# x loaded in place with its gain applied in the splits, a priority on cross output's last tile, and the first retention output weight loaded ahead of its operands

## The chip, the core and the metric

The kernel runs on one core of a Trainium2 chip. The metric is the device time of one execution, in microseconds (us). The kernel before took 2256.48, 2258.14 and 2258.49 us in three runs; the median is 2258.14. The profile is of one more execution.

## What is computed

One inference step of a one-layer encoder, for a prompt of 1024 tokens and a sample of 64, D_MODEL = 1024, in float32:

```
xn = rms_norm(x, g);  xn @ w_in -> retention q|k|v|gate, SWA q|k|v, branch gates A|B
A  = retention(4 heads of 256), per-head norm, swish gate, @ w_ret_out
B  = sliding-window attention (16 heads of 64 on 2 KV heads, window 128), @ w_swa_out
x += (sigmoid(gate_a) * A + sigmoid(gate_b) * B) @ w_mix_out
x += cross_attention(rms_norm(x), memory of 256 tokens, 4 heads)
x += swiglu(rms_norm(x));   y = rms_norm(x)
```

Outputs are y, the retention states, the window's keys and values, and the memory's keys and values, for prompt and sample.

## The kernel before

**Numbers.** Every fp32 matmul operand is split into a hi and a lo part of type fp32r: `split` (L122) casts hi on ACT (L123) and subtracts on DVE for lo (L124). A product is three matmuls: hi x hi, hi x lo, lo x hi. A gain of a norm is one number per row of a transposed activation, that is, one per SBUF partition; `gained` (L269) applies it within a split: ACT multiplies and writes hi, DVE makes x*g - hi with one scalar_tensor_tensor.

**Layout.** Tokens stand in the free dimension: 8 tiles of 128 rows x 1088 tokens. For the projections and the feed-forward network the 1088 tokens are halved (HALF = 544, of 2 x HC = 272), and the products are Strassen's: 7 products (L205, L206, L208 are the matmuls of one) of weight operands P1 to P7 (built on POOL, L183 to L189) and activation operands B11, B12, B21, B22, T1 to T4. `put_op` splits one quarter of x into such an operand, and `put_sum` (L1280) first makes the difference of two quarters on DVE: T1 = B12 - B11, T2 = B22 - T1, T3 = T2 - B11, T4 = B21 - T2. The operands lie in two rings of eight slots. DVE adds the products from PSUM (u, L252).

**Stages.** Start and projections (0 to about 817 us): w_v by plain products, then w_k, w_q and the others by Strassen, with the retention heads (L691 to L815) between them. Mix (817 to 1240): sliding-window attention, and between its steps a filler that first does the last memory values (w_mv), then the retention output, w_ret_out. Cross attention (1240 to 1400), cross output (1400 to 1510), feed-forward (1510 to the end).

**The start** (`start_phase`). The 16 pieces of x (128 x 544) are loaded into four buffers `xr`; ACT multiplies each by its gain g into xg (L428), and with that frees the buffer for the next load. The first two w_v weights are loaded between the pieces. The operands are then split from xg: B11 and B12 after the second group of pieces, B21, B22, T1 (`first_sums`), T2, T3, T4 after the first weight's split. `token_squares` loads x once more for the norm's sums, which DVE adds (L452).

**Cross output** (`cross_out_phase`). For each of 8 rows of tiles and each of 3 chunks of tokens (384, 384, 320): load the residual, 24 matmuls, add the residual on DVE (L1241), store, apply the norm's gain (L1244), square and add the square into the norm's sum (L278). After the last row the norm's roots follow (`some_rstd`, L306).

**The filler** (`filler`). `operands` loads the gated retention outputs (d_gate, eight tiles per chunk) and splits them into `rets`. Each of these loads is pinned with issue_after behind the last weight load at that time (`self.loaded`, set in `unit_raw`). Then come the last memory values with weights that were loaded earlier (`first_units`), then for m = 0 to 7 `unit(w_ret_out[m])`, that is the load into a buffer `raw` (a pool of 2, 128 x 1024 each, shared by all weights), its split, and the products over the three chunks. The window attention's vT is loaded behind `operand_loaded`, the last d_gate load of the first chunk.

**Order.** All loads and stores go through SP's queue (L117), which issues in order. A scheduler at build time chooses each engine's order from the program's dependences and its own estimates; `tc.high_priority()` moves instructions forward in it, `tc.issue_after(i)` holds them behind i. The kernel waits for semaphores where tiles are reused.

Of the kernel before, what the change touches and what calls it, by code (L numbers as in the profile page):

```python
# [2 lines left out]

# [1 line left out]

# [6 lines left out]
F32 = mybir.dt.float32  # L12
F32R = mybir.dt.float32r
AF = mybir.ActivationFunctionType
ALU = mybir.AluOpType
# [4 lines left out]
P = 128  # L20
D = 1024
KT = D // P
# [18 lines left out]
HALF = T // 2  # L41
# [68 lines left out]
class Kernel:  # L110
# [295 lines left out]
    def start_phase(self, ctx):  # L406

        nc, tc, io = self.nc, self.tc, self.io
        g = self.gains[:, 0, :]
        xg = self.ring_tiles(0, KT // 2, "xg", F32)  # L410
        self.xg = [xg[k // 2][:, k % 2, :] for k in range(KT)]
        self.ops, self.slots = {}, {}
        self.new_b12(ctx)
        sp = ctx.enter_context(tc.tile_pool(name="sp", bufs=1, reuse_waits="tile"))
        self.early = [sp.tile([P, 2, HC], F32, name=f"early{i}") for i in range(4)]
        xr = lambda: sp.tile([P, HALF], F32, tag="xr", bufs=4, name="xr")
        raws = [self.wp.tile([P, 1024], F32, tag="raw", bufs=2, name="raw") for i in range(2)]

        def columns(j):
            for i in range(2):  # L420
                self.load(raws[i][:, j * 512:(j + 1) * 512].rearrange("p (k m) -> p k m", m=P), io["w_v"][i][:, 4 * j:4 * j + 4])

        def pieces(k0, t):
            hs = slice(t * HALF, (t + 1) * HALF)
            for k in range(k0, k0 + 4):
                x = xr()
                self.load(x, io["xT"][k, :, hs])
                nc.scalar.mul(self.xg[k][:, hs], x, g[:, k:k + 1])  # L428

        for n, (k0, t) in enumerate(((0, 0), (0, 1), (4, 0), (4, 1))):  # L430
            pieces(k0, t)
            if n < 2:
                columns(n)
            if n == 1:
                self.operands_early()
        self.load(self.ident, io["c_ident"])
        w = self.plain_weights(raws)
        self.operands_late(self.first_sums)
        return w

    def token_squares(self):

# [602 lines left out]
    def filler(self):  # L1045

        nc, tc, io = self.nc, self.tc, self.io
        if True:
            def ld():
                self.lds.append(self.lds.pop(0))  # L1050
                return self.lds[-1]

            rets = self.ring_tiles(1, KT, "ret")

            def operands(c0, n):
                after = self.loaded
                for k in range(KT):
                    a = ld()
                    with tc.issue_after(after):
                        ins = self.load(a[:, :n], self.d_gate[0][k, :, c0:c0 + n])  # L1060
                    if c0 == 0:
                        self.operand_loaded = ins
                    self.split(a[:, :n], rets[k][:, 0, c0:c0 + n], rets[k][:, 1, c0:c0 + n])

            for c0, n in CH:
                operands(c0, n)
            us, h = self.first_units, H - 1
            for t in range(2):
                ps = self.dense_psum()
                for k in range(KT):  # L1070
                    x = self.ms[k][:, :, t * P:(t + 1) * P]
                    self.mm3(ps[:, :256], x[:, 0], x[:, 1], *us[k // 4][k % 4], k == 0, k == KT - 1)
                    if k == 3:
                        yield
                o = ld()[:, :256]
                with tc.high_priority():
                    nc.scalar.mul(o, ps[:, :256], self.mtok[:, t:t + 1])
                self.store(self.d_mv[h, :, t, :], o)
                self.store(io["o_mv"][t * P:(t + 1) * P, h * 256:(h + 1) * 256], o)
                yield  # L1080
            for m in range(KT):
                u = self.unit(io["w_ret_out"][m], KT)
                for c0, n in CH:
                    g = ld()
                    self.load(g[:, :n], self.d_gate[1][m, :, c0:c0 + n])
                    for ps in self.pieces(u, rets, c0, n):
                        if ps is None:
                            yield
                    nc.vector.tensor_tensor(out=g[:, :n], in0=ps, in1=g[:, :n], op=ALU.mult)
                    self.store(self.d_mix[m, :, c0:c0 + n], g[:, :n])  # L1090
                    yield
# [130 lines left out]
    def cross_out_phase(self):  # L1222
        nc, tc, io = self.nc, self.tc, self.io
        with ExitStack() as ctx:
            cq = ctx.enter_context(tc.tile_pool(name="cq", bufs=1, reuse_waits="tile"))
            ctx.enter_context(self.plain_psum(side="right"))
            pn = ctx.enter_context(tc.tile_pool(name="pnc", bufs=1, reuse_waits="tile", space=PSUM, side="right"))
            self.norm_psum = lambda name: pn.tile([P, 512], F32, tag="n", name=name)
            xg = self.ring_tiles(0, KT // 2, "xg", F32)
            self.xg = [xg[k // 2][:, k % 2, :] for k in range(KT)]  # L1230
            self.ops, self.slots = {}, {}
            units = [lambda m=m: self.unit(io["w_co"][m], KT) for m in range(KT)]
            norms, rs = [], []
            for m, u, (c0, n) in self.m_major(units, CH, tail=2):
                if m == 4 and not self.ops:
                    self.operands_early()
                    self.first_sums()
                x = cq.tile([P, 384], F32, tag="hx", bufs=4, name="hx")[:, :n]
                self.load(x, self.d_h[0][m, :, c0:c0 + n])
                ps = self.dense(u, self.couts, c0, n)  # L1240
                nc.vector.tensor_tensor(out=x, in0=ps, in1=x, op=ALU.add)  # L1241
                self.store(self.d_h[1][m, :, c0:c0 + n], x)
                acc = self.rstd_f[:, c0:c0 + n]
                nc.vector.scalar_tensor_tensor(self.xg[m][:, c0:c0 + n], x, self.gains[:, 2, m:m + 1],  # L1244
                                               self.rstd[:, c0:c0 + n], ALU.mult, ALU.mult)
                self.add_square(acc, x, m == 0, cq, n)
                if m == KT - 1:
                    root = self.root[:, c0 // 384, :]
                    def first(acc=acc, root=root):
                        rs.append(self.some_rstd(acc, times=root))  # L1250

                    norms.append((first, lambda acc=acc, i=len(norms): self.spread(acc, rs[i])))
                    if len(norms) < 3:
                        self.later += norms[-1][:3 - len(norms)]
            self.later, self.last_roots = [norms[1][1], norms[2][1]], norms[2][0]
# [39 lines left out]
            b11, b12, _, _ = self.quarters(k)  # L1295
            self.put_sum("T1", k, b12, b12, b11)

    def operands_late(self, sums=None):
        self.op_tiles(1, ("B21", "B22", "T2", "T3"))
        qs = [self.quarters(k) for k in range(4)]  # L1300
        for k, (b11, b12, b21, b22) in enumerate(qs):
            self.put_op("B21", k, b21)
        for k, (b11, b12, b21, b22) in enumerate(qs):
            self.put_op("B22", k, b22)
        if sums is not None:
            sums()
        for k, (b11, b12, b21, b22) in enumerate(qs):
            self.put_sum("T2", k, b12, b22, b12)
        for k, (b11, b12, b21, b22) in enumerate(qs):
            self.put_sum("T3", k, b11, b12, b11)  # L1310
        self.op_tiles(0, ("T4",))
        for k, (b11, b12, b21, b22) in enumerate(qs):
            self.put_sum("T4", k, b21, b21, b12)
# [290 lines left out]
```

## Time and profile before

| | us |
|---|---|
| median of 3 runs | 2258.14 |
| profiled execution, its time | 2251.97 |
| profiled execution, its span | 2250.1 |
| PE busy | 2172.4 |
| DVE busy | 1594.2 |
| ACT busy | 896.2 |
| POOL busy | 689.0 |

The mean granted TensorE clock is 0.988 of full speed. PE is TensorE, DVE is VectorE, ACT is ScalarE, POOL is GpSimd, and SP issues the DMAs; PEq or SPq is an engine's sequencer. A row of a timeline gives start, duration, engine, line, operation, tiles (out<-in), shapes, and in brackets the idle time ahead of it and what ended that. A row of waits gives engine, tile, line, what it waited for, then the sum, the number and the longest. A row of a group by shape gives the sum, the mean in ns, and the idle time ahead. A row of windows gives the busy time and number of instructions of PE, PE's weight loads, DVE, ACT and POOL, the granted clock, the busy share of the DMA engines, and GB/s.

### The profile page before, as it was taken

The page shows a single profiled execution, that of the slowest core. Times are in us where ns is not written, and L with a number is a line of the kernel's source. Part 1 is how long each engine was busy: PE and PEld are TensorE (multiplying, and loading weights), DVE is VectorE, ACT ScalarE, POOL GpSimd, SP SyncE. Part 2 cuts the span into 40 slices and gives each one's busy share as a digit, 9 for nine tenths or more (in the row PEclk, how much of TensorE's full clock was granted, in tenths as well). Part 3 has the DMA queues.
Part 4 walks back from the last instruction along what each step waited for, and adds up shares of the span by engine and source line. Part 5 has one row for each costly group of instructions (what it writes and reads, how often), then busy time and mean ns, then how long its engine had stood idle before and what let it go on. Part 6 is the DMA issues. An engine that isn't in the chain of part 4 may idle for free.

```text
span 2250.1 us, 41674 instructions
## 1 busy us (share of the span) xinstructions
PE 2172.4 (97%) x16382; PEld 2108.2 (94%) x16382; DVE 1594.2 (71%) x2656; ACT 896.2 (40%) x1921; POOL 689.0 (31%) x466
## 2 busy tenths in 40 slices
PE   7899999999999989999999999999999999999996
PEld 6899999999999977779999998999999999999996
DVE  8985878677687568875455565776777767777596
ACT  7333333435444355553233343333222223344344
POOL 1441534342253112220000000014555556434471
PEclk9999999999999989999999999999999999999997
DMA  5433344443445475326343111412342332475223
GB/s 199 159 120 109 111 129 130 132 130 113 169 139 187 143 242 164 111 67 222 121 153 113 39 66 59 143 62 91 122 148 79 101 131 85 152 258 192 86 84 108
DMA packets 182598, 290.84 MB, mean 129 GB/s; under 512 B 40290, under 2 KB 110850, under 8 KB 182402
## 3 DMA queue, kind: packets, MB, share of 16 engines
q1 hardware_dynamic: 177794, 279.26, 38.2%
q10 hardware_dynamic: 4608, 8.91, 1.1%
q8 instruction: 129, 2.11, 0.4%
q14 instruction: 67, 0.55, 0.1%
HBM read 196.95 MB, written 91.16 MB: 128 GB/s over the span
## 4 chain that ended last, share of the span: by engine, by line
PE 80%; DVE 10%; DMA 4%; issue 3%; ACT 2%; POOL 1%; SPq 0%; DVEq 0%; ACTq 0%; POOLq 0%
PE pq L205 15%; PE pq L208 15%; PE pq L206 15%; PE pd L149 8%; PE pd L150 8%; PE pd L151 8%; DVE wq L124 2%; PE pout L992 1%; PE pp L976 1%; DMA hl<-d_op 1%; PE pss L934 1%; DVE T L124 1%; DVE B L124 1%; PE pk L691 1%; DVE xg L1280 1%
## 5 line engine op out<-in xcount | busy, mean ns | idle before, releaser
L123 ACT CAST wq<-raw 128x512 fp32r<-128x512 f32 (+1 forms) x505 | 307.9, 614 | 572.1 <-PE pq L208 308.2
L124 DVE TENSOR_TENSOR wq<-raw,wq 128x512 fp32r<-128x512 f32 (+1 forms) x505 | 447.6, 890 | 107.7 <-ACT wq L123 105.7
L205 PE MATMUL pq<-T,wq 128*128 128x272 f32 x1832 | 501.3, 291 | 6.4 <-DVE u L252 3.1
L206 PE MATMUL pq<-T,wq 128*128 128x272 f32 x1832 | 497.7, 288 | 0.0
L205 PE MATMUL pq<-B,wq 128*128 128x272 f32 x1592 | 436.7, 292 | 11.7 <-ACT wq L123 10.5
L206 PE MATMUL pq<-B,wq 128*128 128x272 f32 x1592 | 435.1, 290 | 9.1 <-DVE B L124 8.9
L208 PE MATMUL pq<-T,wq 128*128 128x272 f32 x1832 | 382.6, 289 | 1.0 <-DVE wq L124 0.9
L183 POOL TENSOR_TENSOR raw<-raw 128x512 f32<-128x512 f32 (+1 forms) x59 | 81.6, 1383 | 899.7 <-DVE wq L124 615.2
L205 PEld LDWEIGHTS pq<-T,wq 128*128 128x128 f32 x1832 | 345.2, 188 | 7.2 <-DVE u L252 3.2
L206 PEld LDWEIGHTS pq<-T,wq 128*128 128x128 f32 x1832 | 348.5, 190 | 0.3 <-issue 0.3
L208 PE MATMUL pq<-B,wq 128*128 128x272 f32 x1592 | 333.5, 289 | 0.0
L206 PEld LDWEIGHTS pq<-B,wq 128*128 128x128 f32 x1592 | 304.4, 191 | 11.7 <-DVE B L124 11.3
L205 PEld LDWEIGHTS pq<-B,wq 128*128 128x128 f32 x1592 | 301.3, 190 | 12.4 <-ACT wq L123 10.5
L208 PEld LDWEIGHTS pq<-T,wq 128*128 128x128 f32 x1832 | 285.3, 188 | 2.4 <-DVE wq L124 1.7
L208 PEld LDWEIGHTS pq<-B,wq 128*128 128x128 f32 x1592 | 249.1, 189 | 0.5 <-issue 0.3
L252 DVE TENSOR_TENSOR u<-pq,u 128x544 f32<-128x544 f32 x177 | 127.7, 721 | 128.2 <-PE pq L208 127.5
L186 POOL TENSOR_TENSOR raw<-raw 128x512 f32<-128x512 f32 (+1 forms) x59 | 83.5, 1415 | 141.0 <-DVE wq L124 133.4
L563 DVE TENSOR_TENSOR stage<-pq,u 128x544 f32<-128x544 f32 x112 | 80.4, 718 | 29.1 <-PE pq L208 26.5
L962 POOL TENSOR_TENSOR t<-t,den 128x768 f32<-128x768 f32 (+2 forms) x34 | 47.9, 1409 | 167.5 <-DVE nm L950 58.7
L184 POOL TENSOR_TENSOR raw<-raw 128x512 f32<-128x512 f32 (+1 forms) x59 | 88.3, 1497 | 3.7
L1438 POOL TENSOR_TENSOR y<-u,y 128x544 f32<-128x544 f32 x38 | 63.0, 1664 | 73.6 <-DVE y L1436 51.8
L189 POOL TENSOR_TENSOR raw<-raw 128x512 f32<-128x512 f32 (+1 forms) x59 | 84.1, 1426 | 4.4
(356 smaller groups left out, 4669.8 us busy)
## 6 DMA issues: line engine op xcount, KB each, us to landing
hl<-d_op SPq DMA_DIRECT2D x85, 272.0 KB, 4.1
d_qkv<-stage SPq DMA_DIRECT2D x44, 272.0 KB, 2.1
d_op<-stage SPq DMA_DIRECT2D x44, 272.0 KB, 2.1
d_op<-ht SPq DMA_DIRECT2D x44, 272.0 KB, 3.3
raw<-w_gate SPq DMA_DIRECT2D x22, 512.0 KB, 3.4
raw<-w_up SPq DMA_DIRECT2D x22, 512.0 KB, 3.5
d_gate<-stage ACTq DMA_DIRECT2D x32, 272.0 KB, 2.3
raw<-w_down SPq DMA_DIRECT2D x16, 512.0 KB, 4.3
```

Of the source, the lines that this page charges most:

```text
L123: self.last_cast = self.nc.scalar.copy(hi, src).ins
L124: self.nc.vector.tensor_tensor(out=lo, in0=src, in1=hi.bitcast(F32), op=ALU.subtract)
L149: mm(ps, wh, xh, start=start, stop=False)
L150: mm(ps, wh, xl, start=False, stop=False)
L151: self.last_mm = mm(ps, wl, xh, start=False, stop=stop).ins
L184: tt(out=a21, in0=a21, in1=a22, op=add)
L186: tt(out=a11, in0=a22, in1=a11, op=sub)
L189: tt(out=a12, in0=a12, in1=a11, op=sub)
L205: mm(ps[:, c, :HC], w[:, 0, ks], x[:, 0, cs], start=start, stop=False)
L206: mm(ps[:, c, :HC], w[:, 0, ks], x[:, 1, cs], start=False, stop=False)
L208: self.last_mm = mm(ps[:, c, :HC], w[:, 1, ks], x[:, 0, c * HC:(c + 1) * HC], start=False, stop=stop).ins
L252: add = lambda out, a, b: nc.vector.tensor_tensor(out=out, in0=a, in1=b, op=ALU.add)
```

## The change

Three edits.

1. The 16 pieces of x are loaded straight into xg, with no `xr` and no multiply of their own. The operands are split by a new function, `start_operands`: hi of B11, B12, B21, B22 is x times the gain (ACT), lo is one scalar_tensor_tensor with the gain (DVE). T1 is the bare difference, times g on ACT in place, then split; T2, T3 and T4 take the gain in their difference (scalar_tensor_tensor, T3 with -g, which one new instruction makes into `gneg`). The pieces and the loads of the constant `ident` come first in the program, then the operands, then the first weight's split. `operands_early` and `operands_late` are left for the feed-forward network, and `operands_late` loses its argument.
2. In `cross_out_phase`, the instructions on the last row of tiles (m = 7) that follow its matmuls are under `tc.high_priority()`.
3. In `filler`, the load of w_ret_out[0] stands ahead of `operands`, and the split of m = 0 takes it from there. As `unit_raw` sets `self.loaded`, the operands' loads are pinned behind this load.

```
@@ start_phase
-        xr = lambda: sp.tile([P, HALF], F32, tag="xr", bufs=4, name="xr")
+        self.gneg = self.np.tile([P, KT], F32, name="gneg")
+        nc.vector.tensor_scalar(self.gneg, g, -1.0, None, ALU.mult)
...
-                x = xr()
-                self.load(x, io["xT"][k, :, hs])
-                nc.scalar.mul(self.xg[k][:, hs], x, g[:, k:k + 1])
+                self.load(self.xg[k][:, hs], io["xT"][k, :, hs])
...
-            if n == 1:
-                self.operands_early()
         self.load(self.ident, io["c_ident"])
-        w = self.plain_weights(raws)
-        self.operands_late(self.first_sums)
-        return w
+        self.start_operands()
+        return self.plain_weights(raws)
+
+    def start_operands(self):
+        nc = self.nc
+        g, stt = self.gains[:, 0, :], nc.vector.scalar_tensor_tensor
+        self.op_tiles(0, ("B11", "T1"))
+        self.ops["B12"] = [self.b12[:, k] for k in range(4)]
+        self.op_tiles(1, ("B21", "B22", "T2", "T3"))
+        self.op_tiles(0, ("T4",))
+        col = lambda t, k: t[:, k:k + 1]
+        qs = [self.quarters(k) for k in range(4)]
+        for i, name in enumerate(("B11", "B12", "B21", "B22")):
+            for k in range(4):
+                o, x, gk = self.ops[name][k], qs[k][i], col(g, k + i // 2 * 4)
+                nc.scalar.mul(o[:, 0], x, gk)
+                stt(o[:, 1], x, gk, o[:, 0].bitcast(F32), ALU.mult, ALU.subtract)
+        for k, (b11, b12, b21, b22) in enumerate(qs):
+            nc.vector.tensor_tensor(out=b12, in0=b12, in1=b11, op=ALU.subtract)
+            nc.scalar.mul(b12, b12, col(g, k))
+            self.put_op("T1", k, b12)
+        for k, (b11, b12, b21, b22) in enumerate(qs):
+            stt(b12, b22, col(g, k + 4), b12, ALU.mult, ALU.subtract)
+            self.put_op("T2", k, b12)
+        for k, (b11, b12, b21, b22) in enumerate(qs):
+            stt(b11, b11, col(self.gneg, k), b12, ALU.mult, ALU.add)
+            self.put_op("T3", k, b11)
+        for k, (b11, b12, b21, b22) in enumerate(qs):
+            stt(b21, b21, col(g, k + 4), b12, ALU.mult, ALU.subtract)
+            self.put_op("T4", k, b21)
@@ filler
+            first = self.unit_raw(io["w_ret_out"][0], KT)
             for c0, n in CH:
                 operands(c0, n)
...
-                u = self.unit(io["w_ret_out"][m], KT)
+                u = self.unit(io["w_ret_out"][m], KT) if m else self.unit_parts(first, KT)
@@ cross_out_phase
-                nc.vector.tensor_tensor(out=x, in0=ps, in1=x, op=ALU.add)
-                self.store(self.d_h[1][m, :, c0:c0 + n], x)
...
+                with tc.high_priority() if m == KT - 1 else nullcontext():
+                    nc.vector.tensor_tensor(out=x, in0=ps, in1=x, op=ALU.add)
+                    self.store(self.d_h[1][m, :, c0:c0 + n], x)
...
@@ operands_late
-    def operands_late(self, sums=None):
+    def operands_late(self):
...
-        if sums is not None:
-            sums()
```

More of the change, by code (lines that the diff above doesn't have):

```diff
@@ L1 @@
 import math
-from contextlib import ExitStack, contextmanager
+from contextlib import ExitStack, contextmanager, nullcontext
 import numpy as np
@@ L1240, in cross_out_phase @@
                 ps = self.dense(u, self.couts, c0, n)
-                nc.vector.tensor_tensor(out=x, in0=ps, in1=x, op=ALU.add)
-                self.store(self.d_h[1][m, :, c0:c0 + n], x)
[L1243 to L1246, printed above, removed]
+                with tc.high_priority() if m == KT - 1 else nullcontext():
+                    nc.vector.tensor_tensor(out=x, in0=ps, in1=x, op=ALU.add)
+                    self.store(self.d_h[1][m, :, c0:c0 + n], x)
+                    acc = self.rstd_f[:, c0:c0 + n]
+                    nc.vector.scalar_tensor_tensor(self.xg[m][:, c0:c0 + n], x, self.gains[:, 2, m:m + 1],
+                                                   self.rstd[:, c0:c0 + n], ALU.mult, ALU.mult)
+                    self.add_square(acc, x, m == 0, cq, n)
                 if m == KT - 1:
```

## The prediction

> **What bounds the kernel now.** I read the page's engine totals first, then its row of 40 slices for PE, then the waits of PE by stretch.
>
> ```profile
> span 2250.1 us, 41674 instructions
> ...
> PE 2172.4 (97%) x16382; PEld 2108.2 (94%) x16382; DVE 1594.2 (71%) x2656; ACT 896.2 (40%) x1921; POOL 689.0 (31%) x466
> ...
> PE   7899999999999989999999999999999999999996
> ```
>
> PE is busy in 97% of the span, so an edit can win only PE's idle time (77.7 us) and its cold clock. The row has dents only at the start, in slice 15 (788 to 844 us) and at the end. The change works at the start, at about 820 to 860, and at 1500.
>
> Waits of PE from 0 to 50, then from 816 to 862 us (total, times, longest):
>
> ```profile
> PE pq L205 <- ACT wq L123: 10.5, 1, 10.5
> PE pq L206 <- DVE B L124: 5.5, 3, 2.6
> ```
> ```profile
> PE pd L149 <- ACT wq L123: 8.6, 2, 5.8
> ```
>
> PE's start waits for the first weight; then three waits for the lo half of an operand from DVE. In the mix stage 5.8 us go before the first retention output matmul. But PE isn't the only engine short of time at the start; the 40-us windows (PE, PEld, DVE, ACT, POOL busy, PE clock, DMA share, GB/s):
>
> ```profile
> 40.00:80.00 40.00, 37.08 (x295) 36.77 (x293) 38.71 (x49) 20.39 (x35) 15.97 (x10) 1.00 0.63 214
> 80.00:120.00 40.00, 35.89 (x274) 35.45 (x275) 38.37 (x75) 15.68 (x32) 17.11 (x11) 0.96 0.36 123
> 120.00:160.00 40.00, 38.62 (x311) 38.24 (x309) 37.01 (x59) 13.83 (x30) 20.84 (x14) 1.00 0.28 95
> ```
>
> The reader is to see the third number: DVE is busy 38.7 and 38.4 of 40 us from 40 to 120, fuller than PE. PE's waits at 80.2 (3.09 us, for DVE u L252) and 98.6 (3.57 us, put down to issue; the transposes of vf want a PSUM bank that DVE L289 frees at 98.2) are DVE's doing.
>
> **Part 1: x in place.** ACT and DVE by shape, in the start:
>
> ```profile
> L428 ACT ACTIVATE xg<-xr,gains 128x544 f32<-128x544 f32 x16 | 11.7, 747 | 0.0
> L123 ACT CAST B<-xg 128x544 fp32r<-128x544 f32 x12 | 7.7, 642 | 0.0
> ```
>
> Sixteen multiplies L428 and sixteen B casts become sixteen multiplies that write hi at once, plus four for T1: 12 ACT operations fewer, 12 x 0.64 = 7.7 us. ACT is 40% busy here, so that frees no bound. What it starts earlier counts: x loads no longer wait for an xr buffer that ACT frees (the last was issued at 23.2), so 16 x 0.279 MB and two weights of 0.52 MB can land by about 20 us at the 260 to 356 GB/s seen there. The first matmul waits for the first cast of a weight, which stands behind eight L428 in ACT's order; I put it at 9 instead of 10.5. On SP the w_k loads (13.8, 15.5) move behind x; w_k is wanted after 50 us.
>
> DVE's count stays: 16 B lo, 16 differences, 16 T lo, of which 28 become a form that reads a gain per partition. Nearest rows: 128x384 with gain 0.619 (L269) against 0.557 without (L278); 128x256 0.477 (L726) against 0.421 (L124 co). So 0.06 each, 28 x 0.065 = 1.8 us more, and 0.7 us for gneg and one rotary operation now ahead of L289. Against it: DVE starts 1.2 us earlier, and gaps of 1.3 (waits for B hi) and 0.7 (at 45.8) close. Net 0.7 us earlier at L289. So the 5.5 us that PE waits at 22 to 34 mostly go, and it then waits for DVE at 80 instead: **that stall is moved, not removed**. What is left comes from PE's order as built: the transposes of vf now stand behind 27 more product matmuls, 27 x 0.126 = 3.4 us, which fill the 3.57 us of idle. The cold clock behind that idle (98.9 to 102.4, pitch 0.228 against 0.126: 15 x 0.1 = 1.5 us) may go with it. Lower end: DVE is later by its 2.5 us and no gap closes, less 1.5 for the first matmul: -1. Upper: 1.5 + 5.5 + 1.5 = 8.5. I take 3.5 of the 0.7 to 5.6 that these steps give: from 120 on DVE has 3 us in 40 to spare, so most of what PE gains at 98 stays.
>
> Between 100 and 800 us the retention heads and projections come in another order on every engine, with the same matmuls; ACT's table loads rise from 19 to 21 (2 x 1.28 us, ACT at 40%). PE's waits of 200 to 800 sum to 3.3 us in all, so little can be won, and a new stall the size of the old ones costs 2: 0, from -2 to +2.
>
> **Part 2: priority on cross output's last tile.** In the order as built, every engine's instructions of that stage stand as before. Cost 0; the 1.15 and 3.65 us waits near 1498 and 1508 stay, with the cold clock behind the second.
>
> **Part 3: w_ret_out ahead.** In the trace:
>
> ```profile
> 831.35 0.81 SPq L117 DMA_DIRECT2D raw<-w_ret_out  x2
> ```
> ```profile
> 837.65 0.69 PE L149 MATMUL pd<-ret,wq 128*128 128x384 f32 x1 [5.79 <-ACT wq L123]
> 838.13 0.52 PE L150 MATMUL pd<-ret,wq 128*128 128x384 f32 x1
> 839.28 0.69 PE L151 MATMUL pd<-ret,wq 128*128 128x384 f32 x1 [0.62 <-DVE wq L124]
> 839.77 0.52 PE L149 MATMUL pd<-ret,wq 128*128 128x384 f32 x1
> ```
>
> The load was issued at 831.35 and its matmul came 6.3 us later; all else of that matmul was there. In the order as built the load goes ahead of the eight d_gate operands on SP. It needs a raw buffer; both hold the last memory weights until DVE's lo at about 821.6. SP takes things in order, and the operands are pinned behind this load (issue_after), so **the added wait holds them too**: they were issued from 809.83 to 823.12, and now start at 821.7. Then come, at the 0.35 MB/us of this stretch (294 to 384 GB/s), 0.52 (weight) + 1.57 (operands) + 1.05 (d_sq) MB = 9.0 us, so 830.7 plus about 2 of latency for the eighth operand; with skv (0.6 MB) vT lands at 834.3 (831.6 before), and the first matmul comes at 834.9 instead of 837.65, without the 0.62 for its lo: 2.8 to 3.4, I take **3.0**. The d_gate loads of the second and third chunk have 5 to 8 us to spare. From 860 PE is full, so it carries. Bounds: +4.5 (no wait but what is left of vT) and -6.7 (rival D).
>
> **A rule against a row.** Before 837.65 PE idled 5.7 us, and then ran at a granted clock of 0.50: pitch 0.32 until 842.6, against 0.173 at 872. Idles of 2.61 (25.6) and 3.09 us (80.2) were followed by the full pitch, 0.126; those of 3.57 (98.6) and 3.65 (1508) by 0.228. My new idle there is 834.9 - 832.0 = 2.9 us. If it stays under 3.1, twelve matmuls win 0.147 each, 1.8 us: rival G. [...] As 2.9 rests on a landing time that I know to 1 us or worse, and the lo wait may add to it, the forecast keeps the cold clock.
>
> **Sum.** -3.5 + 0 + 0 - 3.0 = -6.5: 2251.97 - 6.5 = 2245.5 for the profiled execution, which lies 6.17 under the median of 2258.14; **2251.6** on the median.
>
> **Rivals**, on the median:
> - B, DVE takes all of the start: its rows at 38.4 to 38.7 of 40 say so, the 27 matmuls moved ahead speak against it. -3.0: 2255.1.
> - C, the start pays in full, 8.5: 2258.14 - 11.5 = 2246.6. For it, the stalls are PE's; against it, DVE.
> - D, the other side. SP's hold costs more than the weight gives: in before the eight operand loads took 13.3 us from first to last issue. If that spacing is a limit of the queues and not of the stage's other work, the eighth is issued at 821.7 + 0.5 (the weight's) + 13.3 = 835.5 and vT lands 8.5 us later as before (823.1 to 831.6), at 844.0: first matmul 844.3, **+6.7**. It decides once vT lands after 837.3. With the start's gain 2261.3, without it 2264.8. Against it: in before those loads waited for ld buffers and DMA slots (SP's waits there: d_gate for stage 11.7 us), done by 823.
> - F, the new order of 100 to 820 costs 4 us (two stalls like that at 80, or DVE's later retention): 2255.6; with 8 us, 2259.6. For it, 96 places in PE's order differ; against it, PE's 3.3 us of waits there.
> - G, warm clock at the retention output: -8.3, 2249.8.
> - That the change doesn't do what it says holds for part 2, priced at 0 in every case.
>
> **Numbers.** Forecast 0.34 (2249 to 2254), G 0.13, C 0.09, B 0.14, F 0.13, D 0.17. A measurement can tell about 0.2%, 4.5 us: faster is below 2253.6. Faster: 0.31 + 0.13 + 0.09 + 0.02 = 0.55. Slower, above 2262.6: most of D, 0.13, and the tail of F and of unseen reordering, 0.05. Same: 0.27. The range: 2246 leaves out half of C, 2262.5 the upper part of D and F, 0.2 in all.
>
> **What would show it.** Start: no waits of PE for B lo at 22 to 34, DVE still above 38 of 40 from 40 to 120, the first matmul near 9, vf's transposes without the 3.57. Cross output: the same 1.15 and 3.65. Retention output: w_ret_out issued near 821.7 (less the start's gain), the eighth d_gate some 8 us after it, the first matmul 2.9 us after PE's last work. Wrong if vT lands more than 6 us later than before, or if PE's waits between 100 and 800 exceed 6 us.

## The result and the profile after

The changed kernel takes 2277.44 us (median of 6 runs, 2274.73 to 2278.81); before, run beside it, 2259.95 us (6 runs). The ratio is **1.0074, 95% interval [1.0059, 1.0088]**: slower by 16.7 us (the ratio's distance from 1, times 2258), where 2251.6 and a gain were forecast and 2262.5 was the upper end. The profiled execution took 2276.98 us, with a span of 2275.2.

To see where the time goes I compare the two traces at equal work. The *lateness* of a matmul is its start minus the sum of the usual pitches of all matmuls ahead of it on PE; the table gives after minus before, in us, at some points of PE's work.

| us of PE's work done | 30 | 80 | 110 | 200 | 280 | 340 | 360 | 780 | 820 | 1460 | end |
|---|---|---|---|---|---|---|---|---|---|---|---|
| after | -8.6 | -6.8 | +0.3 | -1.6 | +3.8 | +1.5 | +12.7 | +15.0 | +20.5 | +24.1 | +24.4 |

(The profiled execution of before lies 8 us under the median that the result is taken against, that of after 0.5 us under its own; so the end shows more than 16.7.) The start gains 8.6 us and gives all of it back by 110; some 5 us go between 200 and 280, **11 in one place at 350**, 5 in the mix stage at 800 to 820, and another 3.6 little by little up to 1460. How much two executions differ of themselves is seen from a run reported below, e3, whose order is that of before: its lateness stays within 1.5 us of before's up to 1460.

The start, first. Waits of PE from 0 to 200 us (engine, tile, line, releaser: sum, times, longest), and the windows of 40 us:

```profile
PE pq L205 <- ACT wq L123: 9.8, 3, 9.1
PE pq L205 <- DVE stage L588: 3.6, 1, 3.6
PE pb L840 <- ACT ret_o L836: 3.0, 2, 2.1
PE pq L208 <- DVE wq L124: 2.9, 1, 2.9
PE pq L205 <- DVE u L252: 2.8, 1, 2.8
PE pk L716 <- issue: 0.5, 1, 0.5
```

```profile
40.00:80.00 40.00, 33.65 (x243) 32.91 (x242) 39.99 (x50) 18.53 (x31) 15.41 (x10) 0.92 0.63 201
80.00:120.00 40.00, 35.89 (x272) 35.48 (x271) 39.38 (x72) 13.49 (x26) 19.13 (x12) 0.95 0.34 105
```

The waits for B's lo are gone, the first matmul comes at 9.1, the wait before vf's transposes (now L716) fell from 3.57 to 0.5. But DVE is busy 39.99 of 40 us, and PE waits for it in three other places: at 46.0 for a weight's lo (2.9), at 77.4 for u (2.75), at 106.7 for a stage (3.62). The granted clock is 0.92 and 0.95 there, where before had 1.00 and 0.96.

Then the place at 350. PE, DVE and SP (now with L588, L751 for the lines L563, L726 of before), each from its timeline:

```profile
383.86 0.58 PE L149 MATMUL pkv<-vb,kt 128*128 128x256 f32 x1 [9.33 <-DVE vb L751]
```

```profile
381.03 0.72 DVE L588 TENSOR_TENSOR stage<-pq,u 128x544 f32<-128x544 f32 x1 [11.61 <-DMA d_qkv<-stage]
```

```profile
365.05 0.67 SPq L120 DMA_DIRECT2D d_rb<-rb  x1
365.81 0.60 SPq L120 DMA_DIRECT2D d_qkv<-stage  x1
```

PE waits 9.33 us for a retention value vb from DVE; DVE has vb next but stands at L588, which needs a stage tile; that tile comes free when its store to d_qkv lands; and right ahead of that store, on the same queue, is the store of the bias table, d_rb. Windows of 2 us of the same stretch:

```profile
370.00:372.00 2.00, 2.00 (x18) 2.00 (x17) 0.00 (x0) 0.00 (x0) 0.00 (x0) 1.00 0.84 93
...
374.00:376.00 2.00, 0.53 (x5) 0.30 (x3) 0.00 (x0) 0.00 (x0) 0.00 (x0) 1.00 0.84 93
376.00:378.00 2.00, 0.00 (x0) 0.00 (x0) 0.00 (x0) 0.00 (x0) 0.00 (x0) 0.93 0.91 95
378.00:380.00 2.00, 0.00 (x0) 0.00 (x0) 0.00 (x0) 0.00 (x0) 0.00 (x0) 0.50 0.92 249
```

From 370 DVE, ACT and POOL stand at zero, and from 374.5 PE as well, while the DMA engines are 84% and then 91% busy at only 93 to 95 GB/s: they are full of one slow transfer. In before the same store was issued at 349.85, and the next store to d_qkv only at 361.06:

```profile
349.85 0.67 SPq L120 DMA_DIRECT2D d_rb<-rb  x1
...
361.06 0.33 SPq L120 DMA_DIRECT2D d_qkv<-stage  x1
```

Its 13.4 us to landing (first line below, from the list of transfers) lay where nothing waited for it: PE's waits from 200 to 800 in before are the two that follow.

```profile
d_rb<-rb SPq DMA_DIRECT2D x1, 1024.0 KB, 13.4
```

```profile
PE pb L815 <- ACT ret_o L811: 2.3, 3, 1.2
PE po L151 <- DVE ss L124: 1.0, 2, 0.7
```

Third, the mix stage. PE's waits in after from 816 to 890, and SP at the weight:

```profile
PE pp L1001 <- POOL t L987: 4.7, 1, 4.7
PE pss L959 <- DVE t L972: 2.7, 1, 2.7
PE pd L149 <- ACT wq L123: 1.9, 1, 1.9
PE pd L936 <- DMA swin<-d_skv: 1.5, 1, 1.5
...
PE pd L149 <- ACT swin L938: 0.6, 1, 0.6
```

```profile
838.33 0.34 SPq L117 DMA_DIRECT2D raw<-w_ret_out  x1
838.76 0.86 SPq L117 DMA_DIRECT2D swin<-d_gate  x2
```

The wait of 5.8 us for w_ret_out's cast is gone. In its place stand 2.7, 1.5 and 0.6 for what was loaded behind it, so that the first retention output matmul comes at 852.84, 15.2 us later than in before, and after was 15.0 late already at 780: nothing was won there. Then comes a new wait of 4.7 us for the window's softmax: POOL waits there for DVE, which from 861 to 872 does twelve splits of `ret` between its steps.

### The profile page after: what moved, and what is told of

The parts are those of the page before. It is cut to its first block, busy times and chain, and to the rows that moved or that the text cites. A ratio compares the mean times of both kernels' runs of the same rounds, so it can differ in the third digit from the quotient of the medians.

```text
span 2275.2 us, 41662 instructions
## 1 busy us (share of the span) xinstructions
PE 2188.1 (96%) x16382; PEld 2121.7 (93%) x16382; DVE 1594.6 (70%) x2657; ACT 892.1 (39%) x1911; POOL 695.0 (31%) x466
## 4 chain that ended last, share of the span: by engine, by line
PE 78%; DVE 11%; DMA 4%; ACT 3%; issue 2%; POOL 1%; SPq 0%; DVEq 0%; ACTq 0%; POOLq 0%
PE pq L205 14%; PE pq L208 14%; PE pq L206 14%; PE pd L149 8%; PE pd L151 8%; PE pd L150 8%; DVE wq L124 3%; PE pout L1017 1%; PE pp L1001 1%; DMA hl<-d_op 1%; PE pss L959 1%; DVE stage L588 1%; DMA d_qkv<-stage 1%; DVE T L124 1%; DVE B L124 1%
## 5 line engine op out<-in xcount | busy, mean ns | idle before, releaser
L205 PEld LDWEIGHTS pq<-T,wq 128*128 128x128 f32 x1832 | 351.7, 192 | 12.7 <-issue 4.9
L588 DVE TENSOR_TENSOR stage<-pq,u 128x544 f32<-128x544 f32 x112 | 80.3, 717 | 60.2 <-PE pq L208 40.2
```

Source lines behind the costliest of these rows:

```text
L205: mm(ps[:, c, :HC], w[:, 0, ks], x[:, 0, cs], start=start, stop=False)
L588: nc.vector.tensor_tensor(out=o, in0=ps, in1=sb, op=ALU.add)
```

## The experiments

**Theory A**, from the traces: the new order of the retention puts the table's slow store ahead of the stage stores, and part 3's hold on SP costs a little; the start is worth about nothing, because DVE takes its gain back. **Rival B:** the loss is the held loads of part 3, or (B2) the new order itself, whatever the store does. Each ratio below is to runs of before on the same chip; "us" is the ratio's distance from 1 times 2258.

**The parts alone.** e1: only the edits of `start_phase`, `start_operands` and `operands_late`. e2 and e3:

```
e2  +            first = self.unit_raw(io["w_ret_out"][0], KT)
                 for c0, n in CH: ...
    +                u = self.unit(...) if m else self.unit_parts(first, KT)
e3  +                with tc.high_priority() if m == KT - 1 else nullcontext():
```

> Only x in place (part 1), the other two parts as before. Theory A, from the two traces: the start itself is worth about 0 by 110 us of PE work, and the new order of the retention heads puts the store of the bias table (d_rb, 1 MB in packets of 1 KB) right ahead of the stores of a stage tile, so that DVE and then PE wait (9.3 us, and some 5 us of half clock after it): about +14 us against before, with no loss between 800 and 880. Rival B: the loss is made in the mix stage by the held loads of part 3: then this kernel is within 4 us of before.

> Only the early load of w_ret_out (part 3). Theory A: SP holds the operands behind the load, the first retention output matmul comes no earlier, and a later step of the window attention waits for DVE: about +5 us. What the prediction said: -3 us. Rival: 0, if the loss at 840 to 875 in the changed kernel came only with its other state at 815.

> Only the priority on cross output's last tile (part 2). Its instructions stand in the same order on every engine in that stage, only two DVE instructions at the very end change places: 0 us, within 2 us. Rival: a part of the loss sits behind 1400 us; then +2 or more.

Measured: e1 1.0070 [1.0057, 1.0083], **+15.8 us**; e2 1.0018 [1.0006, 1.0030], +4.1; e3 1.0001 [0.9993, 1.0009], 0. So part 1 holds nearly the whole loss, and not in the start: e1's trace has PE's wait of 9.03 us for vb at 381. Rival B falls. Part 3 is a small loss, part 2 nothing. In e2 the first retention output matmul comes at 840.59, 2.9 us later than in before, and e2 was 2.9 late already at 780: it comes no earlier, as theory A had it. e2's waits from 816 to 880 are like those of after:

```profile
PE pp L976 <- POOL t L962: 5.7, 1, 5.7
PE pd L149 <- ACT wq L123: 2.7, 1, 2.7
PE pss L934 <- DVE t L947: 2.7, 1, 2.7
```

**The bias table on another queue, and in larger packets.**

```
e4  -  self.store(self.d_rb..., rb...broadcast_to([16, 64, 256]))
    +  nc.scalar.dma_start(self.d_rb..., rb...broadcast_to([16, 64, 256]))
e5, e6  rb holds 4 copies (tag "kt", 16 x 1024); store from broadcast_to([16, 16, 1024])
```

> The changed kernel with all three parts, but the store of the bias table (d_rb) goes through ACT's queue instead of SP's; the order of everything else is the same. Theory A1, the stage stores stand behind it in SP's ring: PE's wait of 9.3 us at 384 goes, about -11 to -14 us against the changed kernel. Theory A2, the 16 DMA engines are full with its small packets whatever the ring: the wait shrinks to some 4 to 6 us, about -5 us. Rival B: the wait is not the table's: no change.

> Part 1 alone (as e1), but the bias table's store is made of packets of 4 KB instead of 1 KB: DVE writes four copies of the 16 x 256 table side by side, so the 1 MB takes fewer packets. Theory A2 (the store's time on the DMA engines is what PE waits for): the wait of 9.0 us at 381 and the half clock behind it go, -9 to -12 us against e1, so +4 to +6 against before, which is what the new retention order costs elsewhere. Rival B2 (DVE's and PE's new order makes the wait, whatever the store): no change, +14 to +16 against before.

> Control for e5: the kernel before with the same store in packets of 4 KB. In before the table's 13 us lay under PE work with no transfer due, so theory A2 says 0 +- 2 us. Rival: the store costs before something too; then -3 or more, and e5's gain is not the collision's.

e4: 1.0076 [1.0064, 1.0088], no gain, so the figures of A1 and of A2 (-5 us) both missed. Its wait shrank, but only to 5.5 us:

```profile
379.11 0.58 PE L149 MATMUL pkv<-vb,kt 128*128 128x256 f32 x1 [5.54 <-DVE vb L751]
```

The order in SP's queue is thus not the whole cause (A1 falls): with the store on another queue most of the wait stays. Why the 3.8 us less of waiting did not show in the time is open. e5: 1.0051 [1.0037, 1.0066], some 4 us better than e1 only. It missed for two reasons that its trace shows. The larger packets hardly helped (from e5's list of transfers; e6 has 12.1):

```profile
d_rb<-rb SPq DMA_DIRECT2D x1, 1024.0 KB, 13.0
```

and the table's new buffer is that of kt, so DVE's kt waited for the store instead (PE's wait of 7.6 us for kt at 380). The control e6 shows the same flaw, a wait of 4.0 for kt at 366, and 1.0021 [1.0011, 1.0030]. The pair says nothing on A2 but that packet size is not what makes the store slow.

**The bias table from 128 partitions.**

```
+  small = self.np.tile([32, 16], F32, tag="small", bufs=1, name="small")
+  nc.vector.tensor_copy(table.rearrange("p (h r) -> p h r", r=8), small.unsqueeze(2).broadcast_to([32, 16, 8]))
   (matmul, copy as before, on 128 partitions instead of 16)
+  self.store(self.d_rb.rearrange("h (r i c) -> (h r) i c", r=8, c=256), rb.unsqueeze(1).broadcast_to([P, 8, 256]))
```

> Part 1 alone (as e1), with the same bytes of the bias table stored from 128 partitions (8 rows of each of 16 heads) instead of from 16; DVE spreads the 32 x 16 table first (one small instruction), the place of the store in SP's order is that of e1. In e5 packets of 4 KB left the store at 13.0 us, so it is the 16 partitions that make it slow. Theory A2: the store takes 4 us or less, DVE's wait of 11.3 us for a stage tile and PE's of 9.0 us at 381 shrink to under 2: -9 to -12 us against e1, +3 to +7 against before. Rival B2 (the new order makes the wait): no change against e1.

> Control for e9: before with the table stored from 128 partitions. A2: 0 +- 2 us, since in before nothing waited for those 13 us. Rival: -3 or more.

> The changed kernel, all three parts, with the table stored from 128 partitions. A2 plus the held loads of part 3: -9 to -12 against the changed kernel, that is +5 to +9 against before: e9 plus e2's 4. Rival B2: as the changed kernel, +17.

e9: **0.9959 [0.9947, 0.9971]**, 25 us less than e1; e12: 0.9970 [0.9958, 0.9982], 23 us less than the changed kernel, both far past their forecasts; the control e10: 1.0016 [1.0007, 1.0025], which is 3.6 us more where 0 +- 2 was expected. In e9 the store lands in

```profile
d_rb<-rb SPq DMA_DIRECT2D x1, 1024.0 KB, 4.8
```

4.8 us, and PE's wait for vb from 200 to 420 us is 0.9 in two pieces. The store stands in SP's order where it stood in e1, right ahead of the stage stores, and DVE's wait at the stage tile, 11.31 us in e1, is

```profile
363.89 0.59 SPq L120 DMA_DIRECT2D d_rb<-rb  x1
364.58 1.95 SPq L120 DMA_DIRECT2D d_qkv<-stage  x2
```

```profile
370.14 0.72 DVE L590 TENSOR_TENSOR stage<-pq,u 128x544 f32<-128x544 f32 x1 [1.86 <-DMA d_qkv<-stage]
```

A2 holds at this place, and B2, that the new order makes the wait whatever the store, falls for it. But the gain is twice what the wait explains, and lateness shows the rest everywhere PE is full: e9 wins 6 us from 1460 on, where it does the same as e1.

**Where the weights lie.** In the built programs the weight tiles wq begin at 64 modulo 128 bytes of a partition in before, at 96 in after and e1 (gneg is 32 bytes), at 32 in e9 and e12, at 0 in e10. Four kernels move them with an unused tile, the order of the instructions being unchanged:

```
+  pad = self.np.tile([P, n], F32, name="pad")     (e13: n = 24, e14: 8, e15: 16, e16: 16)
```

> Before, with an unused tile of 96 bytes per partition that moves all weight tiles from 64 to 32 modulo 128; every engine's instructions and their order are the same. Theory P (where the weights start sets the pitch of the matmuls): the 272-column pitch is 0.1228 instead of 0.1252 us, and some 10,000 of them give -10 to -20 us. Rival: the pitch comes from the order or the program of e9, e11 and e12: no change, within 2 us.

> Before, with an unused tile of 32 bytes: weights at 96 modulo 128, as in the changed kernel. Theory P: pitch 0.1257 as there, +3 to +6 us. Rival: no change; then none of the changed kernel's loss comes from the place of its tiles.

> The changed kernel, with an unused tile of 64 bytes: weights at 32 modulo 128; the bias table's store is untouched. Theory P and A2 together: the wait of 9.3 us at 384 stays, the pitch is 0.1228, so -12 to -18 us against the changed kernel, about +2 against before. If only A2 held: no change, +17.

> e9 with an unused tile of 64 bytes: weights at 96 modulo 128 again, as in e1, so that against e1 only the table's store is changed. A2 and P together: the wait at 381 stays away, the pitch is 0.1257 again: +10 to +16 against e9, that is -9 to -12 against e1 and +3 to +6 against before. If A2 alone made e9's gain: as e9, -9 against before.

e13: **0.9949 [0.9935, 0.9964]**; e14: 1.0007 [0.9996, 1.0018], not clear of 1; e15: 1.0019 [1.0010, 1.0029], 12.4 us less than the changed kernel with the wait still there; e16: 1.0022 [1.0012, 1.0031]. Theory P holds in this much: where the tiles lie sets the pitch. The unused tile moves other tiles along with the weights, so that the weights do it is not shown. The window from 1600 to 1700, where PE does nothing but 272-column matmuls without a gap, in before, after and e13, in this order:

```profile
1600.00:1700.00 100.00, 100.00 (x799) 100.00 (x798) 71.78 (x86) 28.73 (x49) 57.76 (x39) 1.00 0.34 114
```

```profile
1600.00:1700.00 100.00, 100.00 (x798) 100.00 (x798) 71.03 (x87) 28.56 (x48) 53.16 (x37) 1.00 0.36 119
```

```profile
1600.00:1700.00 100.00, 100.00 (x810) 100.00 (x809) 73.39 (x87) 29.43 (x49) 56.20 (x39) 1.00 0.34 108
```

PE is at 100.00 of 100 us in all; what differs is how many matmuls that is: 809 or 810 with the weights at 32 (e9, e13, e15), 799 or 798 elsewhere (before, after, e10, e14, e16). From 64 to 96, then, this pitch does not change, where e14's expectation had it change. The 384-column matmuls of the mix stage have another pattern. Between the starts of two of them, 880 to 1240 us, without idle time, lie 0.1741 us in before and 0.1738 in e16, 0.1769 or 0.1770 in after, e1, e10 and e14, and 0.1734 in e9 and e13. There are 1536 of them, so an estimate of what gneg's 32 bytes cost is 1536 x 0.0029 = 4.5 us, just above the 4.1 that e14's interval allows. The traces have 5 us more lateness between 860 and 1460 in e1 and in e10, which can be what e10 has over its forecast.

**e16 against e1**, 1.0070 to 1.0022, is 10.8 us, as A2 said, but it does not isolate the store. The retention heads come in another order from 360 to 610 us, and e16, though at 96 modulo 128 like e1, has the faster 384-column pitch. By lateness, some 9 of the 10.8 us lie at the store, 4 between 860 and 1460, and e16 loses about 2 elsewhere.

**The start and part 3, further.** e7 puts `first = ...` behind `operands(*CH[0])`. e11 is e9 with `nc.gpsimd` for the additions of squares. e8's edit:

```
-                if k:
-                    nc.vector.tensor_tensor(out=acc, in0=acc, in1=x, op=ALU.add)
```

> Part 3 alone, with the early load of w_ret_out placed behind the operands of the first chunk instead of ahead of them: it still waits for a raw buffer, but those eight loads and the window's loads no longer stand behind it. Theory A (SP's hold is what part 3 loses): -2 to -5 us against before, as the first retention output matmul no longer waits 5.8 us for its weight. Rival: the load takes time from the window attention's loads wherever it stands: 0 to +4.

> Part 1 alone with DVE's 14 additions of squares of x (L452 before) left out, so the norm's sum over x is not made: some 11 us less work for DVE between 20 and 100. Theory A3 (DVE is what takes the start's gain back): PE's waits at 45.9, 77.3 and 106.6 shrink or go, and PE is 6 to 10 us ahead of before at its 110th us of work, where it was 0 to 2 ahead. Rival: they stay; then weights or the order, not DVE's amount of work, set them.

> e9 with the 14 additions of the squares of x moved from DVE to POOL (11 us of DVE's time between 50 and 100). A3 (DVE takes back the start's gain): PE is 5 to 8 us ahead of before at its 110th us of work and keeps most of it: -4 to -6 against e9, about 0 against before. Rival: POOL is late with them, the norm's roots come later and the retention starts later: 0 or + against e9.

e8 (one run, 2260.75 us, read by its trace; it leaves the norm's sums out of the work): PE is 5.6 us ahead of before at its 110th us of work, a little under the 6 to 10 expected. The waits at 77 and 107 are gone, that of 2.9 at 46 stays. From 0 to 120:

```profile
PE pq L205 <- ACT wq L123: 9.4, 3, 8.6
PE pq L208 <- DVE wq L124: 2.9, 1, 2.9
PE pss L149 <- ACT qs L123: 2.2, 1, 2.2
PE pk L714 <- issue: 1.8, 1, 1.8
```

This fits A3, that DVE's amount of work takes the start's gain back; but PE's order differs from e1's too, from the 50th us on, so the order is not excluded. e8 shows one thing more. In its order the same slow store is issued at 344.99 and the next d_qkv store at 356.21, as far apart as in before, and though it takes 14.5 us to land, no wait for vb or for a stage is left from 200 to 420. The loss at the store thus needs both: a slow store, and an order that puts stage stores behind it. e11, 0.9975 [0.9964, 0.9987], is 3.6 us worse than e9 and 3.7 us behind before at 110: with that work on POOL the start is later, as its rival said. e7, where -2 to -5 was expected: 0.9999 [0.9990, 1.0008]; with the eight loads freed, the weight's wait is still 3.9 us and the softmax's 3.6. Part 3 gains nothing in either place.

**What beats both kernels most:** e13, before with an unused tile, at 2247.38 us, and e9, part 1 with the wide table, at 2246.96. At equal places of the weights modulo 128, part 1 with the wide store is not seen to be faster than before: e16 against e14 is +0.15%, e9 against e13 +0.10%, and both pairs of intervals overlap.

## Why the prediction was wrong, point by point

| piece | by | us |
|---|---|---|
| the table's store ahead of the stage stores (some 9 by lateness), and the place of the tiles in the 384-column matmuls (some 4), less 2 | e1 to e16 | +10.8 |
| the rest of part 1: start, order of the retention | e16 to before | +5.0 |
| part 3 | after to e1, e9 to e12, e2 | +1, +2.5, +4.1 |
| part 2 | e3 | 0 |
| sum | | +17 to +20 |
| measured | | +16.7 |

**The step that failed** is the third term of the sum, "0, from -2 to +2", for the new order of 100 to 800 us. It was sized by the waits that before had there, 3.3 us in all. Waits of the old order say nothing of a new one: I counted matmuls and table loads and compared PE's order, but not which transfers stood next to which. The trace of before held the row that mattered, one store of 13.4 us to landing, and the order as built had it between two stores of the stage tiles. What the runs showed in the place of "0" is one wait of PE for vb, 9.33 us in after and 9.03 in e1, that with the half clock behind it (0.50 from 378 to 388 in after) makes up some 9 us of the loss. The prediction's own sign for this came true, PE's waits from 100 to 800 sum to 23.4 us against its limit of 6; but the limit was badly set, since before has 6.4 there. Rival F named the stretch and the sign, at 4 or 8 us and 0.13, but not the store.

The first reading, that an edit can win only PE's idle time and its cold clock, fell as well: e13 wins 11.5 us by how fast a busy PE works (810 matmuls from 1600 to 1700 where before has 799). And where it says that ACT is 40% busy at the start, that is the share of the whole execution; from 0 to 40 us ACT was busy 30.85 of 40. No term of the sum used it.

**The start (-3.5)** was wrong, and by the rival given for it, B. Its steps held one by one: first matmul 9.1 (9 forecast), no waits for B's lo, DVE above 38 of 40, vf's wait gone, 0.06 us lost per operation that reads a gain (medians, 0.78 against 0.72). The sum left out that five DVE operations up to 60 us, against three in before, took 1.8 us in place of 0.7 to 0.8, each beside one of POOL's weight sums; that POOL makes them slow was not tested. What failed is the last, that most of it stays because DVE has slack from 120 on: DVE was at 39.99 of 40 until 80, and PE's gain went into new waits at 46, 77 and 107 before that. At its 110th us of work e1 is 1.8 us ahead of before and e9 0.5 behind, where 3.5 ahead was forecast. The further loss of some 5 us from 200 to 280 (five waits of 0.7 to 1.1 us for kt, stage, ret_o and ret_t in the new order) was in no term. Which of the two orders' differences makes it was not isolated; e8, in yet another order, doesn't have it.

**Part 3 (-3.0).** The wait that it takes away was right (5.8 and 0.6 us gone), the hold on SP was right (the load at 838.33 where 821.7 was forecast, 15 us of it the lateness of everything there), and vT was right within 3 us. What failed is the first matmul itself, forecast 2.8 to 3.4 us earlier: in after and in e2 it comes no earlier, as the waits that the weight gave up came back for other loads. Two things were missed: the loads held back make the window's steps late too (2.7 us for t), and the splits of `ret`, once bunched behind their loads, fill DVE while the softmax needs it (4.7 us). The forecast followed the weight and vT and did not ask what else then ends last, at the first matmul and behind it. Rival D's sign was right, with less than its price. The clock stayed cold (0.50 from 849 to 862 in after): of rival G nothing is seen.

**Part 2 (0)** was right.

**A term that was not there:** 32 bytes for gneg move every weight tile. From 64 to 96 that cost at most 4 us (e14's interval), all of it in the 384-column matmuls as far as the traces show, but the same term can be worth 11.5 (e13).

## What to carry to other kernels

When a scheduler reorders a long stage, list its slow transfers first and look at what each is queued beside in the new order: a transfer that was free may now hold a store that an engine's head instruction needs (here one of 13.4 us that nothing waited for in before, and a wait of DVE of 11.61 us in after). Ask of every filled wait what the bottleneck engine will wait for next; here PE's 8.6 us at the start won nothing behind a DVE that was busy 39.99 of 40 us. And before a difference of half a per cent is put down to an edit, check with an unused tile what the place of the tiles alone is worth (11.5 us here, in e13).

## What the hardware showed that was not expected

**Where the tiles begin changes the pace of the matmuls.** The 272-column fp32r matmul, from 1600 to 1980, has a mean pitch, start to start without idle time, of 0.1239 us with weights at 32 modulo 128 (e9, e13, e15) and 0.1256 at 64, 96 and 0 (before, after, e14, e16, e10). The 384-column one has 0.1734 at 32, 0.1741 at 64, 0.1770 at 96 and 0.1769 at 0, but 0.1738 in e16, which is at 96 too. e13 and e14 show both with the order of every engine as in before. Why 32 is the good one stays open, and whether it is the weights or another tile moved with them; e16 shows that the place modulo 128 is not all.

**The store from 16 partitions is slow with packets of 1 KB and of 4 KB:** 1 MB in 13.4 us in before (13.3 to 14.5 in e2, e3, e7, e13 and e14) with packets of 1 KB, 12.1 and 13.0 with 4 KB, against 4.8 from 128 partitions. While the store from 16 runs alone, before and after show 92 to 98 GB/s. What holds a store from 16 partitions at this pace is not shown.

**In these traces the clock drops by a fixed grid, not by the length of an idle.** The prediction took 3.1 us as safe. After has idles of 2.90 (46.0), 2.75 (77.4) and 2.05 us (131.5) that are each followed by 3.4 us at half clock, while 3.09 us in before were not. In both traces the half clock comes in steps of 3.41 us on one grid. Laid on it, the idles of the first 200 us that cost the clock fill 60% or more of one step (2.05 of 3.41 the least), and those of 2.61 and 3.09 that did not fill at most half of any. That is no threshold: in e8 a step filled to about 40% at 40 to 44 us cost the clock too. So a step need not be idle throughout to cost the clock. After has four such drops in its first 140 us, before has one; by half of 3.41 us, an estimate of what each costs a busy PE is 1.7 us.
